# Token mixing of a hybrid decoder trunk: queries ahead of the gating input, wide and narrow products, eight attention calls

## The chip, the cores and the metric

The kernel runs on one core of a Trainium2 chip. A core has engines that work at the same time, each through its own instructions in their order: the TensorE (PE in the profile, its weight loads PEld), the VectorE (DVE), the ScalarE (ACT), the GpSimd (POOL) and the SyncE (SP), which here only issues DMAs. Where an instruction needs something of another engine, it waits for a semaphore, and all that stands behind it on its engine waits too. The metric is the time on the device in microseconds (us), the median of several executions.

## The reference

Two layers; each is an FFN, a token-mixing sub-layer and a second FFN, on 256 rows of 1024 channels in float32. Only the token mixing is touched:

```python
h = rms_norm(x, mix_pre_g[l])
z = h @ w_in[l]
q, k, v, u_s, v_s, g_a, g_b = jnp.split(z, IN_SPLIT_POINTS, axis=-1)
y_attn = sliding_window_attention(q, k, v, attn_sinks[l])
y_sgu = spatial_gating(gelu(u_s), gelu(v_s), sgu_ln_g[l], sgu_ln_b[l], sgu_w[l], sgu_b[l])
merged = (sigmoid(g_a) * (y_attn @ w_attn_branch[l])
          + sigmoid(g_b) * (y_sgu @ w_sgu_branch[l]))
x = x + rms_norm(merged @ w_out[l], mix_post_g[l])
```

The attention has 16 query heads of 64 channels, 2 key heads (8 query heads share one), a causal window of 128 keys, and a sink for each head that adds exp(sink - m) to the denominator. With blocks of 128 rows, the first block of queries sees 128 keys, the second 256. The spatial gating unit normalises gelu(v_s) over its 1024 channels, multiplies it in 8 groups of 128 channels by a lower-triangular 128 x 128 matrix, adds a bias, and multiplies the result by gelu(u_s).

## The kernel before

**Numbers.** Every float32 operand of a large product is kept as two parts in the reduced type fp32r: a high part (ScalarE copies and rounds) and a low part (VectorE subtracts). A product takes three passes: high by high, high by low, low by high. In the tables `xh`, `wh` are high parts, `wl` low ones; `xt` holds both parts of the 256 normalised rows, for each block of 128 channels 256 columns of the high part and then 256 of the low one.

**Weights.** `Stream` loads the weights in units of 128 x 1024 (512 KB) in the order in which they were added, splits them (`high`, line 143, on ScalarE; `lower`, line 152, on VectorE), and keeps up to `AHEAD` = 7 units split ahead of the product that uses them. The DMAs stand in that order on SP's queue.

**Products.** `feature_major` (lines 291 to 299) makes one unit: for each of 8 blocks of channels three products of 256 columns, two with the same weights. `feature_pairs` (from line 311), which the FFNs use, makes two units together: for each block one *wide* product, of 512 columns (the high weights by both parts of the rows, side by side in a PSUM bank), and one *narrow* one, of 256 columns (the low weights by the high part, added to the first half). The two halves of the bank are then added: a copy on ScalarE (line 690), an addition on VectorE (line 691). `row_major` makes a unit with the rows as weights, 12 products of 512 columns.

**Order in a mixing layer** (`Mix.middle`, from line 846). The units of products follow each other as slots: 8 of the gating input u, 8 of the queries q, 8 of the gate gb, 8 of the gating branch's output projection sg, 8 of the gate ga, 8 of the attention's output projection. Each slot has two halves. `at` hangs work into a half; `go` runs a generator whose `yield n` moves its next step n halves on. So `GATING`, `ATTEND` and `GATE` at the top of the file are starting places: the four calls of `gating` start at slots 9 to 12, the six calls of `attend` at halves 27, 32, 38, 44, 50 and 56. All engines get their instructions in the order in which this program issues them; a DVE instruction that waits holds up all later ones.

**Gating** (`gating`, line 740): two groups by four products of the triangular matrix (line 746) into a bank; VectorE adds the bias (750) and multiplies by `ut`, the Gelu of u (753); then the split (755, 757). It reads `vs`, the normalised gelu(v_s), a tile of the pool `n8`, which has two buffers. The other one is `ut`; later `gb` and `so` take the two.

**Attention** (`attend`, line 760): for each key head one call of 8 query heads for the first block, and two calls of 4 heads for the second. A call makes the scores (lines 776 and 777: queries by the keys' high part `kth` and by their low part `ktl`, 128 columns each in the first block, 256 in the second); VectorE adds the mask and takes the row maximum in one instruction for each head (783); ScalarE the exponentials with their sums (796), and those of the sinks (798); VectorE adds and inverts (801, 803); GpSimd multiplies (804); TensorE transposes (813), and the parts are split (207); value products (825, 826); the two halves of the result are added (836, 839) and split (842, 844) into `yah`, `yal`.

**Banks.** PSUM has 8 banks, which `bank()` hands out in turn: a product into a bank waits until what stood there eight banks earlier has been read.

Of the kernel before, what the change touches and what calls it, by code (L numbers as in the profile page):

```python
# [56 lines left out]
ATTEND = (27, 32, 38, 44, 50, 56)  # L57
GATING = (9, 10, 11, 12)
# [5 lines left out]
def trunk(ctx: ExitStack, tc: tile.TileContext, a: dict, out: bass.AP):  # L64
# [226 lines left out]
    def feature_major(o, u, ah, al):  # L291

        wh, wl = st[u]
        for k in range(KD):
            ks = slice(k * P, (k + 1) * P)
            nc.tensor.matmul(o, wh[:, ks], ah[:, k, :], start=(k == 0), stop=False)  # L296
            nc.tensor.matmul(o, wh[:, ks], al[:, k, :], start=False, stop=False)  # L297
            nc.tensor.matmul(o, wl[:, ks], ah[:, k, :], start=False, stop=(k == KD - 1))  # L298
        st.done(u)

# [10 lines left out]
    def feature_pairs(os, us, both):  # L311

        wide = [[(o, st[u][0], flat(both[:, k]), k) for k in range(KD)] for o, u in zip(os, us)]
        narrow = [(o[:, 0:S], st[u][1], both[:, k, 0, :], k) for o, u in zip(os, us) for k in range(KD)]
        todo = [x for w in wide for x in w[:-1]] + narrow + [w[-1] for w in wide]
        for out_, w, x, k in todo:
            nc.tensor.matmul(out_, w[:, k * P:(k + 1) * P], x, start=(k == 0 and x.shape[1] == 2 * S),  # L319
                             stop=(k == KD - 1 and x.shape[1] == 2 * S))  # L320
        for u in us:
            st.done(u)
# [338 lines left out]
    class FFN:  # L661
# [16 lines left out]
        def middle(self, xt, xth, xtl, turn1, early):  # L678
            for _ in range(2):
                self.into.append((new(m8, [P, 8, S], "m8", F32R), new(m8, [P, 8, S], "m8", F32R)))  # L680
            for c in range(FA, FC):
                o = [bank(), bank()]
                us = self.cols[(c - FA) * 2:(c - FA) * 2 + 2]
                feature_pairs(o, us, xt)
# [16 lines left out]
    class Mix:  # L701
        def __init__(self, l):
# [28 lines left out]
        def prepare(self):  # L731
            vs = new(n8, [P, NT, D], "n8")
            vv = new(kvp, [P, NT, NKV, 2, HD], "vv", F32R)
            kth = new(kvp, [P, NKV, S], "kth", F32R)
            self.into = (vs, vv, kth, ktl, gain("sgu_ln_g", self.l), gain("sgu_ln_b", self.l))
# [24 lines left out]
        def attend(self, g, n, heads):  # L760
# [4 lines left out]
            nh = len(heads)  # L765
# [3 lines left out]
            half = nh // 2  # L769
            s = [bank().rearrange("p (a b) -> p a b", a=half) for _ in range(2)]  # L770
            for i in range(half):
                for r in range(2):


                    q_ = qs_[r][:, heads[0] // 2 + i, qs]
                    nc.tensor.matmul(s[r][:, i, :], q_, kth[:, g, 0:nk], start=True, stop=False)  # L776
                    nc.tensor.matmul(s[r][:, i, :], q_, ktl[r][:, g, 0:nk], start=False, stop=True)  # L777
            yield 3
            m = new(tiny2, [P, 8], "m")
            p = new(t4, [P, nh, nk], "t4")  # L780
            mk = mask.rearrange("p a b -> p (a b)")[:, 256 - nk:]
            for i, hd in enumerate(order):
                nc.vector.tensor_tensor_reduce(out=p[:, i, :], in0=s[i // half][:, i % half, :], in1=mk, scale=1.0,
                                               scalar=sinks[:, l, hd:hd + 1], op0=ALU.add, op1=ALU.max,
                                               accum_out=m[:, i:i + 1])
            nm = new(tiny2, [P, 8], "nm")
            nc.vector.tensor_scalar(out=nm[:, :nh], in0=m[:, :nh], scalar1=-1.0, scalar2=None, op0=ALU.mult)
            sk = new(tiny2, [P, 8], "sk")
            nc.vector.tensor_tensor(
                out=sk[:, :nh].rearrange("p (r j) -> p r j", r=2),  # L790
                in0=sinks[:, l, heads[0]:heads[0] + nh].rearrange("p (j r) -> p r j", r=2),
                in1=nm[:, :nh].rearrange("p (r j) -> p r j", r=2), op=ALU.add)
            yield 1
            sm = new(tiny2, [P, 8], "sm")
            for i in range(nh):
# [5 lines left out]
            nc.vector.tensor_tensor(out=dn[:, :nh], in0=sm[:, :nh], in1=sk[:, :nh], op=ALU.add)  # L801
            rd = new(tiny2, [P, 8], "rd")
            nc.vector.reciprocal(rd[:, :nh], dn[:, :nh])  # L803
            nc.gpsimd.tensor_tensor(out=p, in0=p, in1=rd[:, :nh].unsqueeze(2).to_broadcast([P, nh, nk]),  # L804
                                    op=ALU.mult)
            yield 4
            parts = []
            for i0 in range(0, nh, 4):

                for c in range(n + 1):  # L810
                    ps = bank()
                    for i, hd in enumerate(range(i0, i0 + 4)):
                        nc.tensor.transpose(ps[:, i * P:(i + 1) * P], p[:, hd, c * P:(c + 1) * P], ident)  # L813
                    ph, pl = new(t2, [P, 512], "t2", F32R), new(t2, [P, 512], "t2", F32R)
                    split(ph, pl, ps)
                    parts.append((i0, c, ph, pl))
            yield 5
            outs = []
            for i0, c, ph, pl in parts:
                if c == 0:  # L820
                    o = bank()
# [24 lines left out]
        def middle(self, xt, xth, xtl, turn1, early):  # L846
# [24 lines left out]
            def pairs(units, ah, al, evac):  # L871

                for j in range(KD):
# [6 lines left out]
                    if j % 2 == 0:  # L880
                        o = [None]
# [374 lines left out]
```

## Time and profile before

| | us |
|---|---|
| median of three runs | 1174.44 (1174.43 to 1174.59) |
| the profiled execution | 1175.11 |
| its span, from first to last instruction | 1173.1 |
| first mixing layer: queries, gating input, attention | 223.2 to 345.8 in the span |
| the same in the second layer, up to its first half | 802.2 to 885.7 |

The page's second part gives the engines' busy share in 40 equal slices, in tenths:

```profile
PE   9999999999999999999999999999999999999997
PEld 7888888999888888888888888889988888888886
DVE  6768758877787867766576677589778787676752
ACT  6656644657785456555455665455577754555551
POOL 0000000001131000000000000000021220000000
PEclk9999999999999999999999999999999999999999
```

The TensorE is busy from end to end at its full granted clock; VectorE at some 70 to 80% and ScalarE at some 50 to 60% run beside it; GpSimd works almost only in the attention, in slices 10 to 13 and 30 to 34. A busy TensorE need not be at its peak, since its products overlap in the records. The prediction shows the views on which it rests.

### The profile page before, as it was taken

What the parts mean: (1) busy time and instruction counts of PE and PEld (TensorE: products, weight loads), DVE (VectorE), ACT (ScalarE), POOL (GpSimd) and SP (SyncE); (2) the same over time, 40 slices, a digit from 0 to 9 for tenths busy, and PEclk for the clock granted to TensorE, in tenths of its full rate; (3) what the DMA queues carried; (4) which work ended last, traced back from release to release, by engine and by line L of the source; (5) the groups of instructions that cost most, each with busy time, mean ns of one, the idle gap of its engine ahead of it and who ended that gap; (6) DMA issues with size and microseconds to landing.
All of it is one profiled execution on the core that took longest, in us unless ns stands there. A gap on an engine that the chain in (4) does not pass through costs nothing.

```text
span 1173.1 us, 16953 instructions
## 1 busy us (share of the span) xinstructions
PE 1163.8 (99%) x6293; PEld 1006.8 (86%) x6293; DVE 841.9 (72%) x1431; ACT 674.4 (57%) x1151; POOL 57.5 (5%) x42
## 2 busy tenths in 40 slices
PE   9999999999999999999999999999999999999997
PEld 7888888999888888888888888889988888888886
DVE  6768758877787867766576677589778787676752
ACT  6656644657785456555455665455577754555551
POOL 0000000001131000000000000000021220000000
PEclk9999999999999999999999999999999999999999
DMA  7576674555457446557635657645554672565560
GB/s 250 181 251 228 223 253 140 195 173 175 142 178 237 140 141 216 183 196 268 217 108 192 228 190 240 229 141 184 181 168 137 209 232 77 180 202 198 198 210 36
DMA packets 61428, 220.81 MB, mean 188 GB/s; under 512 B 7073, under 2 KB 7073, under 8 KB 61345
## 3 DMA queue, kind: packets, MB, share of 16 engines
q1 hardware_dynamic: 61056, 219.46, 56.0%
q8 instruction: 50, 0.82, 0.3%
q14 instruction: 34, 0.27, 0.1%
q10 hardware_dynamic: 288, 0.27, 0.1%
HBM read 218.65 MB, written 1.05 MB: 187 GB/s over the span
## 4 chain that ended last, share of the span: by engine, by line
PE 99%; ACT 0%; DVE 0%; issue 0%; DVEq 0%; POOL 0%; POOLq 0%
PE mm L289 51%; PE mm L319 34%; PE mm L296 3%; PE mm L297 3%; PE mm L298 3%; PE mm L254 2%; PE mm L813 1%; PE mm L777 1%; PE mm L776 1%; PE mm L746 1%; PE mm L826 0%; PE mm L825 0%; PE mm L1075 0%; PE mm L276 0%; ACT n L1048 0%
## 5 line engine op out<-in xcount | busy, mean ns | idle before, releaser
L152 DVE TENSOR_TENSOR wl<-raw,wh 128x1024 fp32r<-128x1024 f32 x370 | 452.1, 1248 | 87.1 <-ACT wh L143 85.6
L143 ACT CAST wh<-raw 128x1024 fp32r<-128x1024 f32 x370 | 381.3, 1051 | 151.9 <-DMA raw<-in_ffn_w 74.9
L289 PE MATMUL mm<-wh,m 128*128 128x512 f32 x1088 | 341.7, 391 | 0.0
L319 PE MATMUL mm<-xt,wh 128*128 128x512 f32 x1152 | 276.6, 391 | 0.0
L319 PEld LDWEIGHTS mm<-xt,wh 128*128 128x128 f32 x1152 | 211.4, 188 | 40.7
L289 PEld LDWEIGHTS mm<-wh,m 128*128 128x128 f32 x1088 | 204.3, 188 | 42.0
L289 PE MATMUL mm<-wl,m 128*128 128x512 f32 x544 | 211.8, 389 | 0.0
L319 PEld LDWEIGHTS mm<-xt,wl 128*128 128x128 f32 x1152 | 147.7, 191 | 5.6
L319 PE MATMUL mm<-xt,wl 128*128 128x256 f32 x1152 | 149.4, 283 | 0.0
L289 PE MATMUL mm<-wh,xt 128*128 128x512 f32 (+1 forms) x480 | 144.1, 378 | 0.0
L691 DVE TENSOR_TENSOR t<-mm,t 128x256 f32<-128x256 f32 x144 | 61.0, 424 | 101.3 <-ACT t L690 101.0
L289 PEld LDWEIGHTS mm<-wl,m 128*128 128x128 f32 x544 | 102.2, 188 | 20.6
L690 ACT COPY t<-mm 128x256 f32<-128x256 f32 x144 | 52.4, 364 | 88.9 <-PE mm L319 88.8
L289 PEld LDWEIGHTS mm<-wh,xt 128*128 128x128 f32 x480 | 88.4, 188 | 15.9
L289 PE MATMUL mm<-wl,xt 128*128 128x512 f32 (+1 forms) x240 | 87.5, 375 | 0.0
L296 PE MATMUL mm<-xt,wh 128*128 128x256 f32 x256 | 73.3, 286 | 0.0
L298 PE MATMUL mm<-xt,wl 128*128 128x256 f32 x256 | 72.4, 283 | 0.0
L297 PE MATMUL mm<-xt,wh 128*128 128x256 f32 x256 | 72.4, 283 | 0.0
L693 ACT ACTIVATE t<-t 128x256 f32<-128x256 f32 x72 | 30.1, 418 | 46.3 <-DVE t L691 46.3
L289 PE MATMUL mm<-m,xt 128*128 128x512 f32 x216 | 53.6, 393 | 0.0
L289 PEld LDWEIGHTS mm<-wl,xt 128*128 128x128 f32 x240 | 45.2, 188 | 7.9
L804 POOL TENSOR_TENSOR t<-t,rd 128x1024 f32<-128x1024 f32 x12 | 26.0, 2170 | 505.9 <-DVE rd L803 488.3
(154 smaller groups left out, 1091.6 us busy)
## 6 DMA issues: line engine op xcount, KB each, us to landing
raw<-in_ffn_w SPq DMA_DIRECT2D x263, 512.0 KB, 4.4
raw<-in_w_in SPq DMA_DIRECT2D x84, 512.0 KB, 4.1
raw<-in_w_sgu_branch SPq DMA_DIRECT2D x16, 512.0 KB, 3.7
raw<-in_w_attn_branch SPq DMA_DIRECT2D x16, 512.0 KB, 3.6
raw<-in_w_out SPq DMA_DIRECT2D x16, 512.0 KB, 4.5
gain<-in_ffn_post_g SPq DMA_DIRECT2D x4, 512.0 KB, 6.2
gain<-in_ffn_pre_g SPq DMA_DIRECT2D x3, 512.0 KB, 6.4
x<-in_x SPq DMA_DIRECT2D x4, 256.0 KB, 5.2
```

Source lines behind the costliest of these rows:

```text
L143: nc.scalar.copy(h, self.raw[u])
L152: nc.vector.tensor_tensor(out=lo, in0=self.raw[u], in1=f(h), op=ALU.subtract)
L254: nc.tensor.transpose(ps[:, k, :], src[:, (c0 + k) * P:(c0 + k + 1) * P], ident)
L289: nc.tensor.matmul(o, every[i][0], every[i][1], start=start and i == 0, stop=stop and i == 2)
L296: nc.tensor.matmul(o, wh[:, ks], ah[:, k, :], start=(k == 0), stop=False)
L297: nc.tensor.matmul(o, wh[:, ks], al[:, k, :], start=False, stop=False)
L298: nc.tensor.matmul(o, wl[:, ks], ah[:, k, :], start=False, stop=(k == KD - 1))
L319: nc.tensor.matmul(out_, w[:, k * P:(k + 1) * P], x, start=(k == 0 and x.shape[1] == 2 * S), stop=(k == KD - 1 and x.shape[1] == 2 * S))
L690: nc.scalar.copy(y[:, half, :], o[half][:, S:2 * S])
L691: nc.vector.tensor_tensor(out=y[:, half, :], in0=o[half][:, 0:S], in1=y[:, half, :], op=ALU.add)
L693: nc.scalar.activation(y[:, 0, :], y[:, 0, :], AF.Silu)
L804: nc.gpsimd.tensor_tensor(out=p, in0=p, in1=rd[:, :nh].unsqueeze(2).to_broadcast([P, nh, nk]), op=ALU.mult)
```

## The change

- The queries' weights are loaded and multiplied before the gating input's, and both as wide and narrow products by pairs of units (`wide_pairs`, `pair_products`). A pair has two banks, one for each unit, where it had one for both; `sums` adds their halves by two copies on ScalarE and two additions on VectorE for each pair. `feature_major` goes.
- u is copied to `ut` first; one Gelu (`L947`) then takes four of its units. The gating calls follow those Gelus, two by two (`GELU` and `GATING` are now distances in halves). The Gelus so come between the attention's exponentials.
- The low parts and the high part of the keys become one tile `keys` (low, high, low). In the first block one product of 256 columns takes the scores of both parts; VectorE adds the mask to the one half, and the row maximum reads the other half and that sum.
- Eight calls of attention, all of 4 heads, from half 17 to half 60.
- The sink becomes one more column of the scores (a copy on ScalarE), so that its exponential comes into the sum; two small instructions on VectorE and one on ScalarE go for each call.
- The probabilities are normalised on VectorE in place of GpSimd.
- `gb` and `so` get their buffers when first written.

```diff
-ATTEND = (27, 32, 38, 44, 50, 56)
-GATING = (9, 10, 11, 12)
+ATTEND = (17, 23, 29, 35, 41, 47, 54, 60)
+GELU = 1
+GATING = 2
...
+    def pair_products(os, us, chunk):
+        wide = [[(o, st[u][0], flat(chunk(k)), k) for k in range(KD)] for o, u in zip(os, us)]
+        narrow = [(o[:, 0:S], st[u][1], chunk(k)[:, 0, :], k) for o, u in zip(os, us) for k in range(KD)]
+        todo = [x for w in wide for x in w[:-1]] + narrow + [w[-1] for w in wide]
+
+        def product(out_, w, x, k):
+            whole = x.shape[1] == 2 * S
+            nc.tensor.matmul(out_, w[:, k * P:(k + 1) * P], x, start=k == 0 and whole, stop=k == KD - 1 and whole)
+
+        return [lambda x=x: product(*x) for x in todo]
...
+            self.q = [st.add(w[10 + j]) for j in range(KD)]
             self.u = [st.add(w[18 + j]) for j in range(KD)]
-            self.q = [st.add(w[10 + j]) for j in range(KD)]
...
+                    if n == 0:
+                        nc.tensor.matmul(s[r][:, i, :], q_, keys[:, r:r + 2, g, 0:nk], start=True, stop=True)
+                    else:
+                        nc.tensor.matmul(s[r][:, i, :], q_, kth[:, g, 0:nk], start=True, stop=False)
+                        nc.tensor.matmul(s[r][:, i, :], q_, ktl[r][:, g, 0:nk], start=False, stop=True)
             yield 3
...
+            if n == 0:
+                for r in range(2):
+                    nc.vector.tensor_tensor(out=p[:, 2 * r:2 * r + 2, 0:nk], in0=s[r][:, :, 0:nk],
+                                            in1=mask[:, 1:2, :].to_broadcast([P, 2, P]), op=ALU.add)
...
+            nc.scalar.copy(p[:, :, nk:nk + 1].rearrange("p (r j) a -> p r (j a)", r=2),
+                           sinks[:, l, heads[0]:heads[0] + 4].rearrange("p (j r) -> p r j", r=2))
             yield 1
...
-            nc.scalar.activation(sk[:, :nh], sk[:, :nh], AF.Exp)
-            yield 3
-            dn = new(tiny2, [P, 8], "dn")
-            nc.vector.tensor_tensor(out=dn[:, :nh], in0=sm[:, :nh], in1=sk[:, :nh], op=ALU.add)
-            rd = new(tiny2, [P, 8], "rd")
-            nc.vector.reciprocal(rd[:, :nh], dn[:, :nh])
-            nc.gpsimd.tensor_tensor(out=p, in0=p, in1=rd[:, :nh].unsqueeze(2).to_broadcast([P, nh, nk]),
-                                    op=ALU.mult)
+            yield 2
+            rd = new(tiny2, [P, 4], "rd")
+            nc.vector.reciprocal(rd, sm)
+            nc.vector.tensor_tensor(out=p[:, :, 0:nk], in0=p[:, :, 0:nk],
+                                    in1=rd.unsqueeze(2).to_broadcast([P, 4, nk]), op=ALU.mult)
             yield 4
...
+            def sums(o):
+                y = new(t2, [P, 2, S], "t2")
+                for i in range(2):
+                    nc.scalar.copy(y[:, i, :], o[i][:, S:2 * S])
+                yield 1
+                for i in range(2):
+                    nc.vector.tensor_tensor(out=y[:, i, :], in0=o[i][:, 0:S], in1=y[:, i, :], op=ALU.add)
+                yield 1
+                return y
...
-            pairs(self.q, xth, xtl, evac_q)
+            wide_pairs(self.q, evac_q)
+
+            def evac_u(j, o):
+                y = yield from sums(o)
+                nc.scalar.copy(self.ut[:, j:j + 2, :], y)
+                if j % 4 == 2:
+                    us = slice(j - 2, j + 2)
+                    yield GELU
+                    nc.scalar.activation(self.ut[:, us, :], self.ut[:, us, :], AF.Gelu)
+                    for g in (j - 2, j):
+                        yield GATING
+                        yield from self.gating(g)
+
+            wide_pairs(self.u, evac_u)
...
-            gb = new(n8, [P, NT, D], "n8")
-            quads(self.gb, xth, xtl, lambda h, t, o: rows_to(gb, h, t, o))
-            so = new(n8, [P, NT, D], "n8")
+            def place(name):
+                if name not in rows_:
+                    rows_[name] = new(n8, [P, NT, D], "n8")
+                return rows_[name]
+
+            quads(self.gb, xth, xtl, lambda h, t, o: rows_to(place("gb"), h, t, o))
...
+    keys = new(const, [P, 3, NKV, S], "keys", F32R)
+    kth, ktl = keys[:, 1], (keys[:, 0], keys[:, 2])
```

**The TensorE at the first unit after the keys and values** of the first layer. Each row is line, operation, output<-inputs (tiles with their numbers: `mm` a bank, `xt` the rows, `wh` and `wl` a unit's weights), size of the output. Before:

```order
L289 MATMUL mm_2247<-wl_2047,xt_374 128x256
L289 MATMUL mm_2247<-wh_2046,xt_374 128x256
L296 MATMUL mm_2294<-xt_374,wh_2141 128x256
L297 MATMUL mm_2294<-xt_374,wh_2141 128x256
L298 MATMUL mm_2294<-xt_374,wl_2142 128x256
```

With the change, where the unit is the first of the queries:

```order
L291 MATMUL mm_2245<-wl_2046,xt_373 128x256
L291 MATMUL mm_2245<-wh_2045,xt_373 128x256
L313 MATMUL mm_2296<-xt_373,wh_2139 128x512 x7
L313 MATMUL mm_2297<-xt_373,wh_2150 128x512 x7
L313 MATMUL mm_2296<-xt_373,wl_2140 128x256 x8
L313 MATMUL mm_2297<-xt_373,wl_2151 128x256 x8
L313 MATMUL mm_2296<-xt_373,wh_2139 128x512
L313 MATMUL mm_2297<-xt_373,wh_2150 128x512
```

The three products for a block have become two, one of twice the columns, and two units alternate in two banks.

**The TensorE at the first scores of the first layer** (`m` are the queries' two parts, `kth`, `ktl` and `keys` the keys). Before, after the sixth unit of the queries (these four score rows come four times):

```order
L297 MATMUL mm_2737<-xt_374,wh_2536 128x256
L298 MATMUL mm_2737<-xt_374,wl_2537 128x256
L776 MATMUL mm_2801<-kth_2123,m_495_2572 128x128
L777 MATMUL mm_2801<-ktl_13_133,m_495_2572 128x128
L776 MATMUL mm_2802<-kth_2123,m_496_2573 128x128
L777 MATMUL mm_2802<-ktl_14_134,m_496_2573 128x128
```

With the change, inside the fifth pair of units, the first of the gating input (the two score rows come twice):

```order
L313 MATMUL mm_2481<-xt_373,wh_2264 128x512
L313 MATMUL mm_2482<-xt_373,wh_2310 128x512
L313 MATMUL mm_2536<-xt_373,wh_2336 128x512 x7
L313 MATMUL mm_2537<-xt_373,wh_2359 128x512 x5
L773 MATMUL mm_2552<-keys_133,m_453_2292 128x256
L773 MATMUL mm_2553<-keys_133,m_454_2293 128x256
```

Two products of 128 columns have become one of 256, and a call of 4 heads has four of them where a call of 8 heads had 16.

**ScalarE and TensorE at the first copies of the gate gb** (the `n` tile is `gb` in these copies; `t` are the attention's tiles, `wh` a unit's high part). ScalarE before:

```order
L206 CAST t_566_3022<-mm_3017 128x512
L206 CAST t_569_3031<-mm_3026 128x512
L143 CAST wh_3052<-raw_2946 128x1024
L945 COPY n_542_2915<-mm_2926 128x512
L945 COPY n_542_2915<-mm_2927 128x512
L143 CAST wh_3088<-raw_2981 128x1024
```

ScalarE with the change:

```order
L799 ACT_TABLE_LOAD
L799 ACTIVATE t_589_2947,sm_2995<-t_589_2947,nm_2952 128x257 x4
L145 CAST wh_3003<-raw_2876 128x1024
L753 CAST m_451_2290<-t_600_3000 128x512
L955 COPY n_606_3015<-mm_2837 128x512
L829 COPY t_611_3037<-mm_2973 64x256 x2
L955 COPY n_606_3015<-mm_2838 128x512
L145 CAST wh_3046<-raw_2919 128x1024
```

And the TensorE with the change, at the last gating product of the layer, which reads `n_409`, the tile whose buffer `n_606` takes:

```order
L291 MATMUL mm_3018<-wh_2784,xt_373 128x512 x2
L291 MATMUL mm_3018<-wl_2785,xt_373 128x512
L291 MATMUL mm_3018<-wh_2784,xt_373 128x512
L744 MATMUL mm_3066<-wt_653,n_409_2120 128x128 x4
L291 MATMUL mm_3017<-wh_2821,xt_373 128x512
L291 MATMUL mm_3017<-wl_2822,xt_373 128x512
```

Before, the gating products stood before the queries' end, and gb's copies had a free buffer. Now the first of those copies (`L955`, issued before slot 20) needs the buffer that the last gating products (issued in slot 21, two units of gb and one call's scores later) still read.

More of the change, by code (lines that the diff above doesn't have):

```diff
@@ L289, in passes @@
             nc.tensor.matmul(o, every[i][0], every[i][1], start=start and i == 0, stop=stop and i == 2)
[L291 to L299, printed above, removed]
     def row_major(o, u, m, ah, al):
@@ L768, in attend @@
             qs = rows_of(n)
-            half = nh // 2
-            s = [bank().rearrange("p (a b) -> p a b", a=half) for _ in range(2)]
-            for i in range(half):
+            s = [bank().rearrange("p (a b) -> p a b", a=2) for _ in range(2)]
+            for i in range(2):
                 for r in range(2):
                     q_ = qs_[r][:, heads[0] // 2 + i, qs]
-                    nc.tensor.matmul(s[r][:, i, :], q_, kth[:, g, 0:nk], start=True, stop=False)
-                    nc.tensor.matmul(s[r][:, i, :], q_, ktl[r][:, g, 0:nk], start=False, stop=True)
@@ L782, in attend @@
+            yield 3
+            m = new(tiny2, [P, 4], "m")
+            p = new(t4, [P, 4, nk + 1], "t4")
+            if n == 0:
+                for r in range(2):
+                    nc.vector.tensor_tensor(out=p[:, 2 * r:2 * r + 2, 0:nk], in0=s[r][:, :, 0:nk],
+                                            in1=mask[:, 1:2, :].to_broadcast([P, 2, P]), op=ALU.add)
             for i, hd in enumerate(order):
-                nc.vector.tensor_tensor_reduce(out=p[:, i, :], in0=s[i // half][:, i % half, :], in1=mk, scale=1.0,
-                                               scalar=sinks[:, l, hd:hd + 1], op0=ALU.add, op1=ALU.max,
+                part = s[i // 2][:, i % 2, :]
+                nc.vector.tensor_tensor_reduce(out=p[:, i, 0:nk], in0=part[:, P:2 * P] if n == 0 else part,
+                                               in1=p[:, i, 0:nk] if n == 0 else mask.rearrange("p a b -> p (a b)"),
+                                               scale=1.0, scalar=sinks[:, l, hd:hd + 1], op0=ALU.add, op1=ALU.max,
@@ L785, in attend @@
                                                accum_out=m[:, i:i + 1])
[L786 to L792, printed above, removed]
+            nm = new(tiny2, [P, 4], "nm")
@@ L817, in attend @@
[L817 to L821, printed above, removed]
-                    outs.append((i0, o.rearrange("p (a b) -> p a b", a=4)))
+            for c in range(n + 1):
+                ps = bank()
+                for i in range(4):
+                    nc.tensor.transpose(ps[:, i * P:(i + 1) * P], p[:, i, c * P:(c + 1) * P], ident)
+                ph, pl = new(t2, [P, 512], "t2", F32R), new(t2, [P, 512], "t2", F32R)
+                split(ph, pl, ps)
+                parts.append((c, ph, pl))
@@ L824, in attend @@
+            yield 6
+            o = bank()
+            for c, ph, pl in parts:
                 v = vv[:, c, g].rearrange("p r d -> p (r d)")
@@ L908, in middle @@
             self.ysh, self.ysl = new(m8, [P, G, S], "m8", F32R), new(m8, [P, G, S], "m8", F32R)
-            for i, slot in enumerate(GATING):
-                at((slot, 0), lambda i=i, slot=slot: go(self.gating(2 * i), 2 * slot))
-            def to(dst, j, o, func=AF.Copy):
-                nc.scalar.activation(dst[:, j:j + 2, :], o, func)
-                yield from ()
-            pairs(self.u, xth, xtl, lambda j, o: to(self.ut, j, o, AF.Gelu))
             self.qs = new(m8, [P, KD, S], "m8", F32R), new(m8, [P, KD, S], "m8", F32R)
@@ L977, in merge @@
                 nc.vector.tensor_tensor(out=y, in0=o, in1=ga[:, t, b], op=ALU.mult)
-                nc.gpsimd.tensor_tensor(out=y, in0=y, in1=so[:, t, b], op=ALU.add)
+                nc.gpsimd.tensor_tensor(out=y, in0=y, in1=place("so")[:, t, b], op=ALU.add)
                 yield 4
@@ L1032, in trunk @@
                             base=0, pattern=[[-1, P]], channel_multiplier=1)
-    ktl = [new(const, [P, NKV, S], f"ktl{r}", F32R) for r in range(2)]
+    keys = new(const, [P, 3, NKV, S], "keys", F32R)
+    kth, ktl = keys[:, 1], (keys[:, 0], keys[:, 2])
     for k in ktl:
```

92 lines of the change are left out of this document (38 added, 54 removed).

## The prediction

> **What bounds the kernel now.** I read the page first (busy time and the chain that ended last), then what the TensorE waited for, then the chain in order of time.
>
> ```profile
> PE 1163.8 (99%) x6293; PEld 1006.8 (86%) x6293; DVE 841.9 (72%) x1431; ACT 674.4 (57%) x1151; POOL 57.5 (5%) x42
> PE 99%; ACT 0%; DVE 0%; issue 0%; DVEq 0%; POOL 0%; POOLq 0%
> PE mm L1075 <- POOL ident masks.py:199: 1.4, 1, 1.4
> PE mm L289 <- ACT n L1048: 0.4, 1, 0.4
> PE mm L289 <- ACT m L143: 0.2, 1, 0.2
> ```
>
> The first line is busy time and share of the span, the second the chain's share by engine; the last three are everything the TensorE waited for (total, times, longest, in us). All three waits lie at the kernel's start; in both token-mixing layers it waits for nothing. So the time is a sum of TensorE products. A change can gain only through the number of products and their spacing, and lose only by a wait that is not there now. Busy time can't tell the spacing, since pipelined products overlap; the chain in order of time can (start, length, what, in us).
>
> ```profile
> 49.72 83.50 PE mm L319 x480
> 249.34 0.89 PE mm L746 x8
> 253.11 0.89 PE mm L746 x8
> 275.80 8.19 PE mm L289 x36
> 294.94 0.87 PE mm L813 x8
> 297.55 5.55 PE mm L289 x24
> 306.73 0.87 PE mm L813 x8
> 308.57 5.46 PE mm L289 x24
> ```
>
> The first row is the FFN, which already works by wide and narrow products (512 and 256 columns): 83.50 us for 240 of each, 0.348 us for one of each. Between the two gating rows lies one unit of the gating input's or the queries' product, 24 products of 256 columns: 253.11 - 249.34 - 0.89 = 2.88 us, 0.120 each. The 512-column row gives 8.19 / 36 = 0.2275 each. Between the transposes that end at 295.81 and the row at 297.55 stand 16 score products of 128 columns: 1.74 us, 0.109 each; between 307.60 and 308.57 stand 8 of 256 columns: 0.97 us, 0.121 each. So a product of 128 columns costs nearly as much as one of 256.
>
> **The change, part by part: TensorE.** (1) Queries and gating input: 2 layers x 16 units x 8 blocks = 256 blocks. Three products of 256 columns (3 x 0.120 = 0.360 us) become one wide and one narrow (0.348 us, the FFN row): 256 x 0.012 = **-3.1 us**. (2) First scores (first query block): 64 products of 128 columns (64 x 0.109 = 7.0 us) become 32 of 256 columns (32 x 0.121 = 3.9 us): **-3.1 us**. The new product reads two pieces of 128 keys; no row shows that reading. Its bounds are 0.120 (one piece, no loss) and 0.218 (as two of 128, no gain); I take 0.121, since its column count is the one of that row. (3) Transposes, value products, gating products and all else keep number and size. Two more attention calls for each layer make a dozen more seams; at the seams shown the rows join within 0.02 us (284.94 + 0.87 = 285.81 at transposes, 275.80 + 8.19 in the row above), so I add 0.1 us.
>
> On the tensor engine a page speaks against this change. The Trainium skill, TensorE: Matmul & The Clock Gate, section "Back-to-back issue gap", gives the isolated gap of two products as N/2.4 + 2.5 ns, 56 ns for 128 columns and 109 ns for 256; by it (1) gains 256 x 2 ns = 0.5 us and (2) 32 x 3 ns = 0.1 us, an estimate from that page. The 0.109 us of the 128-column rows here disagree with its 56 ns, and the 0.120 us are 11 ns above its 109; the rows decide.
>
> **VectorE and ScalarE, which get the rest.** Everything else is added on two engines that now hide behind the TensorE.
>
> ```profile
> 223.20:306.70 83.50, 83.50 (x601) 78.74 (x600) 66.23 (x136) 50.74 (x102) 7.33 (x3) 1.00 0.54 178
> 306.70:345.80 39.10, 39.10 (x198) 33.11 (x197) 32.79 (x58) 32.18 (x64) 12.02 (x7) 1.00 0.44 143
> L691 DVE TENSOR_TENSOR t<-mm,t 128x256 f32<-128x256 f32 x144 | 61.0, 424 | 101.3 <-ACT t L690 101.0
> L753 DVE TENSOR_TENSOR t<-t,n 128x512 f32<-128x512 f32 x4 | 2.8, 692 | 0.1
> L839 DVE TENSOR_TENSOR t<-mm,t 64x512 f32<-64x512 f32 x4 | 2.8, 688 | 1.8 <-ACT t L836 1.7
> L839 DVE TENSOR_TENSOR t<-mm,t 64x256 f32<-64x256 f32 x6 | 2.5, 415 | 0.0
> L801 DVE TENSOR_TENSOR dn<-sm,sk 128x4 f32<-128x4 f32 x4 | 0.6, 156 | 0.0
> 309.26 1.22 DVE L152 TENSOR_TENSOR wl<-raw,wh 128x1024 fp32r<-128x1024 f32 x1
> 311.63 2.31 DVE L152 TENSOR_TENSOR wl<-raw,wh 128x1024 fp32r<-128x1024 f32 x1
> 310.96 1.90 POOL L804 TENSOR_TENSOR t<-t,rd 128x1024 f32<-128x1024 f32 x1 [9.35 <-DVE rd L803]
> ```
>
> The two window rows cover queries, gating and attention of the first layer (length, then busy time of TensorE, its weight loads, VectorE, ScalarE, GpSimd): VectorE 66.23 + 32.79 = 99.0 of 122.6 us (81%), ScalarE 50.74 + 32.18 = 82.9 us (68%). Then come groups (count | busy, mean ns). VectorE gets, for each layer: 16 sums of 256 columns, 16 x 0.424 = 6.8; 8 mask additions of the same size, 3.4; the normalisation that leaves GpSimd, 4 x 0.692 + 4 x 1.22 = 7.6; the output sums in smaller pieces, 16 x 0.415 - 4 x 0.688 - 8 x 0.415 = +0.6; it loses 12 small additions of 0.16 and gets four small ones more, about -1.2. Together **+17 us**. Against that, the split that ran beside the GpSimd multiplication took 2.31 in place of 1.22 us; six such overlaps a layer go, between -3 (were only half a split met) and -6 us. So VectorE comes to 110 to 113 of the 119.5 us that are left, **92 to 95%**.
>
> ```profile
> L690 ACT COPY t<-mm 128x256 f32<-128x256 f32 x144 | 52.4, 364 | 88.9 <-PE mm L319 88.8
> L945 ACT COPY n<-mm 128x512 f32<-128x512 f32 x8 | 4.5, 587 | 0.7 <-PE mm L289 0.7
> L836 ACT COPY t<-mm 64x256 f32<-64x256 f32 x6 | 2.2, 368 | 0.1
> L143 ACT CAST wh<-raw 128x1024 fp32r<-128x1024 f32 x370 | 381.3, 1051 | 151.9 <-DMA raw<-in_ffn_w 74.9
> 331.16 1.28 ACT L955 ACT_TABLE_LOAD   x1
> 332.45 1.06 ACT L955 ACTIVATE n<-n 128x1024 f32<-128x1024 f32 x1
> ```
>
> ScalarE gets 16 copies of 0.364 (5.8 us), about 2 us more for the gating input (four copies of 512 columns and two wider Gelus for four Gelus), and table loads: Gelu, exponential and sigmoid now alternate, and its order holds 21 loads inside the layers in place of 9, six more a layer, 6 x 1.28 = 7.7 us; with small pieces +17, so 100 of 119.5 us (84%). The Trainium skill, ScalarE: Activation LUTs, section "What ACT_TABLE_LOAD costs", adds a drain of about 1.38 us to each switch, which would make it 16 us a layer and ScalarE 91% busy (an estimate from that page). The rows disagree: the load that starts at 331.16 ends at 332.44, and the activation starts at 332.45.
>
> Neither engine's work adds time as long as each result is there when the TensorE wants it. So I followed the new order of the three engines, and looked for the places where a product wants something soon after its cause. Most have over 2 us to spare. The tightest is the one that the order rows in the section on the change show: ScalarE's first copy of the gb product writes into the buffer of the normalised gating input, so it now waits for the last gating product, which stands later in the TensorE's order. ScalarE stands still until then, and what it has behind that copy starts only there. From the end of that gating product the TensorE has 12 products (2.73 us), four value products (0.91), eight transposes (0.87), 12 products (2.73) and four merged scores (0.48) before it wants the bank of that gating product again: 7.7 us.
>
> ```profile
> L783 DVE CUSTOM_DVE_ANT_0 t<-mm,mask,sinks 128x128 f32<-128x128 f32 x16 | 4.5, 348 | 0.1
> L750 DVE TENSOR_TENSOR t<-mm,sb 128x512 f32<-128x512 f32 x4 | 2.8, 690 | 4.8 <-PE mm L746 4.8
> 308.06 1.29 DVE L207 TENSOR_TENSOR t<-mm,t 128x512 fp32r<-128x512 f32 x2 [2.43 <-ACT t L206]
> ```
>
> In that time ScalarE does the copy (0.59), two output copies (0.74), the second gb copy (0.59) and a split (1.05): 2.97 us; then VectorE its half of that split (1.22), two mask additions (0.85), four row maxima (4 x 0.348 = 1.39), a negation (as the small additions, 0.16) and the bias addition that empties the bank (0.69): 4.32. Together 7.3 us: it fits with 0.4 us to spare. Sooner, 2.73 + 0.91 + 0.44 = 4.1 us after the release, a transpose wants the bank of an attention output: 0.59 + 0.74 + 0.83 = 2.2 us, 1.9 to spare. VectorE is not much behind today (the last row: it ends the first split of the transposes that end at 307.60 by 309.35), but will be later by some microseconds where it is 95% busy. So I allow a few short waits: **+0.5 us** for both layers, from 0 (all fits) to 3 (0.75 us at two places in each layer).
>
> DMA: the same loads, queries' before the gating input's, on the same queue; splits run up to seven units of 2.8 us ahead, so a late load or split by a few microseconds is not seen. The masks' and keys' setup lies before the first layer, beside the FFN.
>
> **Sum.** -3.1 - 3.1 + 0.1 + 0.5 = -5.6 us. The profiled execution took 1175.11 us, 2.0 more than its span of 1173.1; it becomes 1169.5. The median of the three runs is 1174.44, 0.67 below it: **1168.8 us**.
>
> **Rivals.**
> - *A: more waits.* VectorE at 95% falls behind, and the TensorE waits 1 to 2 us in each layer, at the seams around the gating products and the transposes. For it: it has up to 17 us more for each layer. Against: its own idle time is mostly waiting for the TensorE today, and the margin is seven units for weights. -6.1 + 2 to 4: 1170.3 to 1172.3.
> - *B: the merged scores give nothing*, if two pieces of 128 keys cost as two products (0.218): -2.5 us, 1171.9.
> - *C: the change doesn't do what it says.* Were the cost by columns alone (0.2275 / 2 = 0.114 for 256, 0.057 for 128), neither form would gain: 3 x 0.114 and 0.2275 + 0.114 are the same. Then +0.6 us: 1175.0. Against: the 0.109 and the 0.348 rows. The page's gap above leads to nearly the same.
> - *D: slower, by ScalarE's copy that waits for a later product.* From the first gb copy's place in the order to the end of the last gating product the TensorE does 24 products, four scores and four gating products: 5.46 + 0.48 + 0.89 = 6.8 us, in which ScalarE stands. If nothing of it were covered, that is 2 x 6.8 = 13.6: 1174.44 - 6.1 + 13.6 = 1182. It decides once VectorE and ScalarE come to that place over some 6 us late; below 0.4 us it costs nothing, and between, the excess. Against: seven units of weights are ahead, and by the sums above they come there 2 to 3 us late.
>
> **How the numbers follow.** Forecast (waits of 0 to 1.2 us, 1168.2 to 1169.7) 0.60; A 0.19; B 0.05; C 0.03; D and A together beyond +8.5 us (over 1176.8) 0.07; smaller losses of D (1172 to 1176.8) 0.02; faster than 1168.2 (scores or seams cheaper than the rows) 0.04. A measurement of this kernel tells about 0.2%, 2.35 us, from no change: faster means below 1172.1, slower above 1176.8. Faster: 0.60 + 0.04 + most of A and B, 0.84; same 0.09; slower 0.07. The range 1167.5 to 1172.2 holds the forecast, A and B.
>
> **What would show it right or wrong.** In the chain of the changed kernel: pairs of units in 5.57 us in place of 5.76; merged scores 0.48 us for four; the TensorE's waits still only at the start; the six table loads more a layer at 1.28 us each; VectorE over 90% busy in the windows of both layers; ScalarE waiting at the first gb copy for a gating product, some 4 us. Wrong: a TensorE wait for VectorE at a gating product or a transpose, a merged score at 0.2 us, a gap before the first products of a pair.

## The result and the profile after

The changed kernel takes **1168.5 us** (median of 5 runs, 1168.06 to 1169.49) against 1174.54 (5 runs): ratio 0.9948, 95% interval 0.9936 to 0.9959, 6.0 us less. 1168.8 was predicted. The profiled execution took 1168.46 us with a span of 1166.7.

The page after (busy time and share of the span), and all that the TensorE waited for:

```profile
PE 1157.3 (99%) x6005; PEld 989.5 (85%) x6005; DVE 864.4 (74%) x1491; ACT 704.6 (60%) x1215; POOL 33.2 (3%) x30
```

```profile
PE mm L1091 <- POOL ident masks.py:199: 1.4, 1, 1.4
PE mm L291 <- ACT n L1064: 0.4, 1, 0.4
PE mm L256 <- DVE t L509: 0.2, 1, 0.2
PE mm L291 <- ACT m L145: 0.2, 1, 0.2
```

Three of the waits lie at the kernel's start, and the one of 0.2 us at 192, ahead of the first layer's part that the change touches; neither token-mixing layer has one in the part that it touches. So the kernel is still a sum of TensorE products, 288 fewer of them (6293 to 6005).

To see a layer by itself, I take the stretch from the first transposition of the keys' work, ahead of the queries' and gating input's products, to the first long row of the next FFN. Everything that the change touches on the TensorE lies in it. The chain of waits before (start, length, what):

```profile
217.38 0.22 PE mm L438 x2
...
443.68 83.54 PE mm L319 x480
...
796.35 0.22 PE mm L438 x2
...
1022.66 83.54 PE mm L319 x480
```

and after, with a row of the queries' products and one of the first scores:

```profile
217.06 0.22 PE mm L437 x2
...
231.44 16.70 PE mm L313 x96
248.14 0.47 PE mm L773 x4
...
440.48 83.54 PE mm L313 x480
...
792.80 0.22 PE mm L437 x2
...
1016.28 83.54 PE mm L313 x480
```

The stretch took 226.30 and 226.31 us before; it takes 223.42 and 223.48 after: **-2.88 and -2.83, together -5.71 us**. The sum on record had -5.6. The profiled executions differ by 6.65 us; the other 0.9 lies outside these layers, half of it (0.48) at the start, where the first FFN's long row begins at 49.24 in place of 49.72. In the runs below this row begins between 49.2 and 50.1 whatever the kernel, so no part of the change is read from there.

In the row of 96 products 48 wide and 48 narrow products take 16.70 us, 0.348 a pair, as forecast; in the next, four merged scores take 0.47, 0.118 each (0.121 was forecast).

The window of the first layer after (length, then busy time of TensorE, its weight loads, VectorE, ScalarE, GpSimd), ScalarE's table loads in the whole kernel, and its wait at gb's first copy:

```profile
223.20:343.00 119.80, 119.80 (x652) 103.43 (x651) 107.56 (x218) 95.40 (x192) 6.78 (x4) 1.00 0.54 172
```

```profile
L799 ACT ACT_TABLE_LOAD x8 | 10.3, 1283 | 0.4
L947 ACT ACT_TABLE_LOAD x4 | 5.1, 1283 | 0.1
L970 ACT ACT_TABLE_LOAD x4 | 5.1, 1283 | 0.1
```

```profile
ACT n L955 <- PE mm L744: 1.1, 1, 1.1
```

VectorE is busy for 107.6 of 119.8 us (90%; 110 to 113 were forecast), ScalarE for 95.4 (80%; 100 were forecast). The wait that the change adds on ScalarE is 1.1 us in the layer, where some 4 had been named.

### The profile page after: what moved, and what is told of

It reads as the page before. It is cut to its first block, busy times and chain, and to the rows that moved or that the text cites. A ratio compares the mean times of both kernels' runs of the same rounds, so it can differ in the third digit from the quotient of the medians.

```text
span 1166.7 us, 16473 instructions
## 1 busy us (share of the span) xinstructions
PE 1157.3 (99%) x6005; PEld 989.5 (85%) x6005; DVE 864.4 (74%) x1491; ACT 704.6 (60%) x1215; POOL 33.2 (3%) x30
## 3 DMA queue, kind: packets, MB, share of 16 engines
HBM read 218.65 MB, written 1.05 MB: 188 GB/s over the span
## 4 chain that ended last, share of the span: by engine, by line
PE 98%; DVE 1%; ACT 1%; DMA 0%; issue 0%; DVEq 0%; POOL 0%; POOLq 0%; ACTq 0%
PE mm L291 50%; PE mm L313 42%; PE mm L256 2%; PE mm L811 1%; PE mm L744 1%; PE mm L821 0%; PE mm L820 0%; DMA raw<-in_w_in 0%; PE mm L777 0%; PE mm L776 0%; PE mm L1091 0%; PE mm L773 0%; DVE wl L154 0%; ACT m L145 0%; PE mm L278 0%
## 5 line engine op out<-in xcount | busy, mean ns | idle before, releaser
L313 PE MATMUL mm<-xt,wh 128*128 128x512 f32 x1408 | 340.2, 391 | 0.0
L313 PEld LDWEIGHTS mm<-xt,wh 128*128 128x128 f32 x1408 | 257.6, 188 | 48.9
L313 PEld LDWEIGHTS mm<-xt,wl 128*128 128x128 f32 x1408 | 180.5, 191 | 6.9
L313 PE MATMUL mm<-xt,wl 128*128 128x256 f32 x1408 | 182.6, 283 | 0.0
L291 PEld LDWEIGHTS mm<-m,xt 128*128 128x128 f32 x216 | 39.7, 188 | 8.7 <-ACT xt L578 1.0
L209 DVE TENSOR_TENSOR m<-t,m 128x256 fp32r<-128x256 f32 x72 | 30.2, 419 | 13.5 <-ACT m L208 13.5
L216 ACT ACTIVATE t<-mm 128x512 f32<-128x512 f32 x24 | 14.3, 598 | 40.9 <-PE mm L291 40.5
L154 DVE TENSOR_TENSOR m<-raw,m 128x1024 fp32r<-128x1024 f32 x20 | 25.8, 1329 | 13.5 <-ACT m L145 13.5
```

Source lines behind the costliest of these rows:

```text
L154: nc.vector.tensor_tensor(out=lo, in0=self.raw[u], in1=f(h), op=ALU.subtract)
L209: nc.vector.tensor_tensor(out=lo, in0=src, in1=f(h), op=ALU.subtract)
L216: nc.scalar.activation(junk, src, AF.Square, accum_out=parts[:, h:h + 1])
L291: nc.tensor.matmul(o, every[i][0], every[i][1], start=start and i == 0, stop=stop and i == 2)
L313: nc.tensor.matmul(out_, w[:, k * P:(k + 1) * P], x, start=k == 0 and whole, stop=k == KD - 1 and whole)
```

## The experiments

Theory: the time is the sum of the TensorE's products (queries and gating input -3.1, first scores -3.1), and all else only has to be in time. Rivals: the gain comes from the new order; or VectorE's and ScalarE's added work, or ScalarE's new wait, costs something that hides in the sum. All times are medians; the kernel before ran beside each group at 1174.55 to 1174.73. The stretch is the one defined above, first and second layer, as the difference to the changed kernel's; it is read from the one profiled execution of each run, which need not be the median one (e8_vec1's took 1174.12 us, the longest of its ten).

| run | us | runs | first | second | sum |
|---|---|---|---|---|---|
| before | 1174.54 | 5 | +2.88 | +2.83 | +5.71 |
| changed | 1168.5 | 5 | 0 | 0 | 0 |
| e1_two_halves | 1171.91 | 9 | +1.50 | +1.52 | +3.02 |
| e2_two_scores | 1172.57 | 11 | +1.78 | +1.79 | +3.57 |
| e3_neither | 1175.44 | 11 | +3.24 | +3.22 | +6.45 |
| e4_u_first | 1186.74 | 4 | +8.85 | +8.80 | +17.66 |
| e5_narrow192 | 1167.66 | 1 | -0.43 | -0.28 | -0.72 |
| e5_narrow64 | 1168.12 | 1 | -0.37 | -0.56 | -0.93 |
| e7_gating1 | 1169.16 | 4 | +0.83 | +0.23 | +1.05 |
| e7_gelu2 | 1171.3 | 8 | +1.03 | +1.03 | +2.06 |
| e8_vec1 | 1172.39 | 10 | +1.87 | +2.53 | +4.39 |
| e8_vec2 | 1185.68 | 4 | +8.72 | +8.16 | +16.88 |
| e9_pool | 1169.85 | 4 | +0.52 | +0.42 | +0.94 |
| e10_close | 1188.11 | 4 | +10.36 | +9.13 | +19.49 |

### The two kinds of products, undone one by one

**e1_two_halves**, the wide product as two of 256 columns:

```diff
...
+            if whole and halves_:
+                for c in range(2):
+                    cs = slice(c * S, (c + 1) * S)
+                    nc.tensor.matmul(out_[:, cs], w[:, k * P:(k + 1) * P], chunk(k)[:, c, :], start=k == 0 and c == 0,
+                                     stop=k == KD - 1 and c == 1)
+                return
...
```

> The changed kernel with each wide product of queries and gating input (512 columns) issued as two of 256 columns; all else, the sums on ScalarE and VectorE too, stays. If the time is the sum of the TensorE's products, 256 blocks x (2 x 0.120 - 0.2275) = +3.2 us: 1171.7 us, 1.6 us in each token-mixing layer, and no TensorE wait there. Rival, the gain came from the new order and not from the form of the products: within 0.5 us of 1168.5.

**e2_two_scores**, the merged first score as two of 128 columns:

```diff
-                        nc.tensor.matmul(s[r][:, i, :], q_, keys[:, r:r + 2, g, 0:nk], start=True, stop=True)
+                        for c in range(2):
+                            nc.tensor.matmul(s[r][:, i, c * P:(c + 1) * P], q_, keys[:, r + c, g, 0:nk], start=True,
+                                             stop=True)
```

> The changed kernel with each merged first score (256 columns over two key parts) issued as two products of 128 columns into the two halves of the same bank; the mask additions stay. Product sum: 32 x (2 x 0.109 - 0.118) = +3.2 us: 1171.7 us. Rival, cost by columns alone: two products of 128 columns cost as much as one of 256, so within 0.3 us of 1168.5.

**e3_neither**, both edits.

> Both edits together: the changed kernel's order, calls and work on the other engines, with the products of before in number and length (only the n=0 scores and the q and u blocks). Product sum: +6.4 us: 1174.9 us, beside the kernel before within 0.6 us, so that order and calls are worth nothing by themselves. Rival, the order is worth something: below 1173. Rival, the added work of VectorE costs something by itself: above 1176.

Measured in the layers: +3.02, +3.57, and +6.45 for both, which is nearly their sum (6.59). The forecasts of the product sum, 3.2, 3.2 and 6.4, hold within 0.4 us, and none of the rivals of e1 and e2 does. The chain of e2 shows the price of the short products:

```profile
248.55 0.84 PE mm L774 x8
```

Eight products of 128 columns take 0.84 us where four of 256 take 0.47. For the eight calls with merged scores that is 8 x 0.37 = 3.0 us; the other 0.6 of e2's 3.57 lies outside the score rows and was not traced. e3 is the important one: the changed kernel's order and its whole added work, with the old products, stands 0.74 us above the kernel before in the layers (6.45 - 5.71), 0.37 in each, a little over the 0.6 allowed. By the median it is 1175.44 against 1174.73, a ratio of 1.0004 (0.9995 to 1.0012), an interval that holds no change too. So order and added work give nothing and cost about 0.7 us in the layers, and the two kinds of products give all of the gain.

### What a narrow product costs at least

**e5_narrow192** and **e5_narrow64** cut the narrow products:

```diff
...
-        narrow = [(o[:, 0:S], st[u][1], chunk(k)[:, 0, :], k) for o, u in zip(os, us) for k in range(KD)]
+        narrow = [(o[:, 0:n], st[u][1], chunk(k)[:, 0, 0:n], k) for o, u in zip(os, us) for k in range(KD)]
...
```

> The changed kernel with the narrow products of queries and gating input cut from 256 to 192 columns (leaves out a quarter of the low part's contribution). Floor theory: a product costs at least the 0.109 us of the 128-column rows; 256 x (0.120 - 0.109) = -2.8 us, spacing 0.109. By columns (a line through 0.120 at 256 and 0.2275 at 512: 0.0125 + 0.00042 x N): 0.093 each, -6.9 us.

> The same with 64 columns (leaves out three quarters of the low part's contribution). Floor theory: again 0.109 each, -2.8 us. By columns: 0.039 each, -20.7 us, or as far as VectorE and ScalarE let it.

The chain of waits with 192 columns, then with 64, at the place where the changed kernel has 16.70 us:

```profile
230.97 16.32 PE mm L313 x96
```

```profile
230.93 16.33 PE mm L313 x96
```

A pair takes 0.340 us in both: less the wide product's 0.2275, the narrow one takes **0.1125 us with 192 columns and with 64**, against 0.1204 with 256. The floor theory stands, and cost by columns (0.093 and 0.039) is out. The floor is what made the old first scores dear. The Trainium skill, TensorE: Matmul & The Clock Gate, section "LDWEIGHTS (loading the stationary operand)", gives a weight load as columns / 1.2 ns, 107 ns for 128 columns; the floor here, 105 to 113 ns, agrees with it. No run here changed the weights' width, so that the weight load is the cause is not shown.

The time did not follow. 256 products times 0.008 us are 2.0 us, but the layers became only 0.7 to 0.9 shorter. The starts of the products, compared one by one with the changed kernel's, show where most of the rest stayed in the first layer: with 192 and with 64 columns, 0.25 and 0.34 us are lost at 264.9 and 0.19 and 0.24 at 286.6, at products that take over a bank in which scores were. There the TensorE now arrives before VectorE is done. This was the first sign of a margin that the prediction had not listed.

### How much more VectorE can take

**e8_vec1** and **e8_vec2** add one or two multiplications by ones behind each normalisation:

```diff
+            nc.vector.tensor_tensor(out=p[:, :, 0:nk], in0=p[:, :, 0:nk],
+                                    in1=ones[:, 0:4].unsqueeze(2).to_broadcast([P, 4, nk]), op=ALU.mult)
```

> The changed kernel with each normalisation followed by one more VectorE multiplication of the same tile by ones (4 x 1.22 + 4 x 0.69 = 7.6 us a layer): VectorE comes to about 115 of 119.8 us (96%), and the chain from exponentials to transposes is 0.7 to 1.2 us longer, where the least margin at a transpose is 1.8 us. My theory: what counts is the margin at the place and not the share; short waits, 0 to 1 us a layer: 1168.5 to 1170.5. Rival (busy share decides): above 95% it falls behind by some us in each layer, 1171 to 1175.

> Two such multiplications (15.2 us a layer): VectorE would have 122.8 us of work in 119.8, so it must fall behind, if only the weights' seven units of lead don't take up the 3 us. Either theory: waits at transposes, gating products and scores, 2 to 6 us a layer: 1172 to 1180.

e8_vec1 gave 1172.39, outside my theory's range and in that of its rival. But the loss in the first layer does not come in many places: of 1.87 us, 1.29 are lost at one product, the first of gb's second four units, one of the two places that e5 had shown; 0.39 lie ahead of two transposes further on. The second row maximum of VectorE there in the changed kernel, and the product (start, length, engine, line, operation), from its timeline:

```profile
285.54 0.48 DVE L788 CUSTOM_DVE_ANT_0 t<-mm,mask,sinks 128x256 f32<-128x256 f32 x1
...
286.64 0.48 PE L291 MATMUL mm<-wh,xt 128*128 128x512 f32 x1
```

and the chain of e8_vec1 at the same place, where the TensorE has its only named wait in that layer (1.0 us):

```profile
288.06 0.40 DVE t L788
...
288.52 3.04 PE mm L291 x12
```

The product writes the bank that the first two row maxima read. (Counted through the program, that bank was given out seven banks before this product's, not eight as the section on the kernel has it. The places of the waits here fit a bank being given out again in the order in which its last reader was issued.) In e8_vec1 it starts at 288.52, 0.06 us after the second maximum ends (288.06 + 0.40). In the changed kernel the second maximum ends at 285.54 + 0.48 = 286.02; the product could start at 286.08 and does at 286.64: **0.56 us to spare**. The added multiplication nearest ahead of it (1.22 us) and what earlier ones left over push VectorE past that. So most of the first layer's loss is decided at one place, and not at one of the transposes that I had named; the rival's number came, but not by falling behind everywhere. e8_vec2 falls behind at transposes too and loses over 8 us a layer, above the 2 to 6 expected (1185.68 in place of 1172 to 1180). A part of this is the clock, below.

**e9_pool** puts the normalisation back on GpSimd:

```diff
-            nc.vector.tensor_tensor(out=p[:, :, 0:nk], in0=p[:, :, 0:nk],
+            nc.gpsimd.tensor_tensor(out=p[:, :, 0:nk], in0=p[:, :, 0:nk],
                                     in1=rd.unsqueeze(2).to_broadcast([P, 4, nk]), op=ALU.mult)
```

> The changed kernel with the normalisation back on GpSimd. VectorE loses 7.6 us a layer and its splits that run beside a multiplication slow to about 2.3 us (+3 to 6 us a layer): 102 to 106 of 119.8 us busy. Nothing waited before, so the time can only stay, 1168.5, or rise by waits at the transposes, since GpSimd's multiplication of 1024 elements takes 1.9 us in place of 1.23 and the least margin there is 1.8 us: within 0.6. Rival: less work on VectorE gains time, below 1167.5.

It is 0.94 us longer in the layers and 1.35 by the median, above the 0.6 expected. In the first layer's comparison 0.49 of 0.52 us lie at the same product at 286.6. VectorE's weight splits in that layer, after and in e9:

```profile
L154 DVE TENSOR_TENSOR wl<-raw,wh 128x1024 fp32r<-128x1024 f32 x38 | 46.5, 1227 | 4.6 <-ACT wh L145 4.4
```

```profile
L154 DVE TENSOR_TENSOR wl<-raw,wh 128x1024 fp32r<-128x1024 f32 x38 | 49.2, 1301 | 7.1 <-ACT wh L145 6.8
```

38 splits cost 2.7 us more beside GpSimd. In the whole kernel VectorE is busy for 5.3 us less (859.1 against 864.4) although 15.3 us of multiplications left it (2 x (4 x 1.226 + 4 x 0.692)). So the edit that moved the normalisation to VectorE cost VectorE only a third of its own length.

### ScalarE's copy that waits for a later product

**e7_gating1** issues the gating products sooner:

```diff
-GATING = 2
+GATING = 1
```

> Each gating product one half-unit sooner after the Gelu, the second of a group two halves: the last gating product now stands ahead of the place where ScalarE comes to its first gb copy. My theory: ScalarE's wait of 1.1 us in each layer goes, and the time stays, 1168.5 within 0.6 us, because that wait hides. Rival: the wait costs its length, 1166.3.

**e7_gelu2** issues the Gelus, and two of a layer's four gating products, later:

```diff
-GELU = 1
+GELU = 2
```

> Gelu and gating products one half-unit later (2.73 us of the TensorE's work): ScalarE's first gb copy waits some 3.8 us in place of 1.1, and everything behind it comes that much later. The nearest things that the TensorE wants behind it have 0.7 (the last gating product's bank) and 1.5 us to spare (the attention output's bank); so it should wait 1 to 2 us in each layer: 1170.5 to 1172.5, the wait named at a transpose or at the first product into that bank. Rival, the rest of the slack takes it up: 1168.5 within 0.6.

In e7_gating1 the wait at the gb copy is gone from ScalarE's list, and the time is not better: 1169.16, just above the 0.6 allowed (+1.05 in the layers) and away from the rival's 1166.3. The TensorE has a new wait of 0.6 us in the first layer, where a gating product wants a bank of scores sooner. So the 1.1 us of ScalarE are not shown to cost anything, as the changed kernel's TensorE, which waits for nothing in that part, had already said.

e7_gelu2 gave 1171.3, in the range of my theory, with 1.03 us more in each layer; but the edit does not do what I expected of it. `GELU = 2` moves the first and the third gating product of a layer behind one more unit; the second and the last stay between the same two units as before. So ScalarE's wait for the last one grew to 1.7 us only (3.8 were expected). The chain in the first layer, from the last gating product's end at 294.26 on:

```profile
294.29 0.59 ACT n L955
...
295.28 0.37 ACT t L829
...
295.66 0.59 ACT n L955
296.25 0.53 ACT m L753
...
296.80 0.70 DVE m L755
...
297.95 0.44 DVE t L832
...
298.44 0.66 PE mm L811 x4
```

That is rival D as the prediction drew it: gating product, gb copy, output copy, the work behind them, and at the end transposes that want the bank of an attention output. What moved is the copy at 296.25 (`L753`), the high part of the third gating product's result: it stood ahead of the first gb copy and now stands behind both, so VectorE waits for it before the output's sum (`L832`). The transposes lose only 0.26 us by this. Of the layer's 1.03 us, 0.43 are lost at the score bank of 286.6 and 0.30 at the first products of sg, so most of this run's loss isn't shown to be D's.

### Order and spacing of the calls

**e4_u_first**, gating input ahead of the queries, and the calls five half-units apart:

```diff
-ATTEND = (17, 23, 29, 35, 41, 47, 54, 60)
+ATTEND = (25, 30, 35, 40, 45, 50, 55, 60)
...
+            self.u = [st.add(w[18 + j]) for j in range(KD)]
             self.q = [st.add(w[10 + j]) for j in range(KD)]
-            self.u = [st.add(w[18 + j]) for j in range(KD)]
...
-            wide_pairs(self.q, evac_q)
...
             wide_pairs(self.u, evac_u)
+            wide_pairs(self.q, evac_q)
```

> The changed kernel's products, but gating input ahead of the queries as before, and the eight attention calls five half-units apart (first at 25, last at 60) in place of six. My theory: the order gives nothing as long as nothing waits; 1168.5 within 0.7 us, TensorE waits in a layer below 0.4 us. Rival: queries first and even spacing are what keeps VectorE in time; then the calls that are closer together make the TensorE wait 1 to 3 us in each layer, at transposes or scores: 1170.5 to 1174.5.

This was the largest miss: +17.7 us in the layers where I expected none, and far above the 1 to 3 us a layer of the rival. The two edits in it were then separated by **e10_close**, which leaves the queries first:

```diff
-ATTEND = (17, 23, 29, 35, 41, 47, 54, 60)
+ATTEND = (25, 30, 35, 40, 45, 50, 55, 60)
...
-GATING = 2
+GATING = 1
```

> Queries first as in the changed kernel, gating products as in e7_gating1 (1169.2 us), and the attention calls of e4_u_first (first at half-unit 25, five apart). Theory 1, closeness: late and close calls put more work of VectorE and ScalarE into a shorter stretch, whatever stands first; then the TensorE waits at transposes and scores as in e4_u_first, 7 to 9 us in each layer: 1183 to 1188. Theory 2, order: what hurt in e4_u_first is that queries come second, so that their evacuation falls among the first calls; then this kernel loses little: 1168.5 to 1171. Between 1172 and 1182 both have a part.

1188.11, just above theory 1's 1183 to 1188, against 1169.16 for e7_gating1: calls that start later and stand closer cost 19 us by themselves, so theory 1 stands, and the order of queries and gating input is not what hurt. The later start and the closer spacing were not tried apart. The TensorE's longest waits in the first layer of e4 (e10 has the first and the third of them too):

```profile
PE mm L811 <- DVE t L804: 3.6, 1, 3.6
PE mm L773 <- ACT n L955: 1.1, 1, 1.1
PE mm L811 <- DVE m L788: 1.1, 1, 1.1
```

And e4's window of the layer, with a piece of its chain:

```profile
223.20:352.00 128.80, 122.85 (x654) 104.85 (x653) 110.23 (x218) 90.90 (x187) 6.78 (x4) 0.99 0.52 164
```

```profile
296.31 2.08 ACT t L799 x8
298.40 0.48 ACT t L208
...
300.99 1.23 DVE wl L154
...
304.73 0.76 DVE t L784 x2
...
306.07 0.66 PE mm L811 x4
```

VectorE is busy for 110.2 of 128.8 us, 86%, less than in the changed kernel, and yet the TensorE waits. The chain says why: exponentials of one call, the split of another call's transposes, the split of a unit of weights, the mask additions of a third, and only then the transposes that the TensorE wants. A call takes 23 half-units from its scores to its last subtraction (the steps of `attend` added up), so nearly five are under way at five apart and not quite four at six apart, on two engines that each work in order.

## Why the prediction was right

1. *TensorE bound, no waits in these layers.* Held, before and after.
2. *Wide and narrow, -3.1 us.* Undoing the wide products costs 3.02 in the layers. The step from the FFN's row (0.348) to these units was exact.
3. *Merged scores, -3.1 us.* Undoing them costs 3.57, of which 3.0 lie in the score rows; a merged score took 0.118, not 0.121. That a product may read two pieces of keys at no loss, which no row had shown, is shown now; rivals B and C are out.
4. *Seams +0.1, waits +0.5.* Together 0.74, from e3 against the kernel before. That this comes near the forecast's 0.6 is luck: no wait is listed in these layers, neither after nor in e3. It lies in small pieces, which were not located one by one; what they are stays open.
5. *Sum -5.6 in the layers.* -5.71. A part of the closeness is luck too: undone together, the two kinds of products are worth 6.45, not 6.2, and the costs 0.74, not 0.6. The median moved by 6.0; the rest lies outside these layers, or within the 1.4 us over which the runs of the changed kernel spread.
6. *Work on the other engines.* Twelve more table loads at 1.28 us and ScalarE's wait for the gating product came as named. VectorE's and ScalarE's sums were some 2 to 5 us too high a layer, and the wait was 1.1 us in place of 4, since ScalarE came to that copy later than I had placed it.
7. *The tightest place.* Here a step failed without harm to the number. I had put the least margin, 0.4 us, at the bank of the last gating product. The timeline after has the bias addition that empties it and the product that takes it:

```profile
299.93 0.69 DVE L748 TENSOR_TENSOR t<-mm,sb 128x512 f32<-128x512 f32 x1
...
301.31 0.40 PE L291 MATMUL mm<-wh,m 128*128 128x512 f32 x1
```

   It is empty at 300.62: 0.7 to spare. The bank of scores at 286.6, which I had not listed, has 0.56; it gave way in e8_vec1 and e9, and in e5 together with the one at 264.9. "Most have over 2 us to spare" was too kind: e8_vec1 costs 4.4 us with 7.6 us of work a layer.
8. *Rivals A and D.* Neither came, and both are near: A with e8_vec1, D's chain with e7_gelu2. That the new starts and spacing of the calls keep the waits away (e10_close: +19 us) the prediction did not say; it had costed that part of the change at nothing.

## What to carry to other kernels

Where one engine bounds a kernel with no wait, take its gain as (products x spacing), from rows of the same shape in the same trace, and then undo each part alone: here e1 and e2 add up to e3. Look for products that stay at the floor (0.11 us below 256 columns here) and merge them. The cover on the other engines is not a busy share but a margin at each bank; find the least one with a run that adds a little work to the covering engine, before something that depends on it (here the starts and spacing of the calls) is moved.

## What the runs showed of the hardware beside that

A wait of the TensorE can cost more than its length. After the 3.6 us wait in e4 the granted clock (the column behind GpSimd's) falls to half, and the next 12 products take 4.26 us where 2.73 are usual:

```profile
345.61 4.26 PE mm L291 x12
```

```profile
346.00:347.00 1.00, 1.00 (x4) 0.81 (x3) 1.00 (x2) 0.97 (x1) 1.00 (x1) 0.50 0.03 8
```

In e8_vec2 the same follows two waits of 0.7 and 1.5 us that lie within 3 us:

```profile
PE mm L291 <- DVE m L788: 1.5, 1, 1.5
PE mm L815 <- DVE t L836: 0.7, 1, 0.7
```

```profile
289.58 4.54 PE mm L291 x12
```

```profile
290.50:292.50 2.00, 2.00 (x6) 1.52 (x6) 2.00 (x5) 1.88 (x4) 0.00 (x0) 0.50 0.56 229
```

After the single 1.0 us wait of e8_vec1 the clock stays at 1.00. The Trainium skill, TensorE: Matmul & The Clock Gate, section "What's actually happening", has the clock fall to half after an idle window of about 3.4 us. The 3.6 us of e4 agree. In e8_vec2 the TensorE was idle for only 2.2 us in two pieces, and the clock fell as well. Between and just ahead of the pieces it ran nothing but transposes: from the end of its last value product at 286.32 to 289.58, 3.3 us, it did eight of them and no other product. So short waits may add up, or transposes may not count as work; no run here tells the two apart.
